# Attention scores as three products of 64 rows in the two halves of TensorE's rows

## The chip, the cores and the metric

The kernel runs on one core of a Trainium2 chip. The metric is the device time of one execution in microseconds (us). TensorE (PE in the profile, PEld for its weight loads) multiplies, VectorE (DVE), ScalarE (ACT) and GpSimd (POOL) do the rest, and all data transfers are issued from the queue of SyncE (SP, SPq).

## The reference, cut to what matters

One layer of a decoder trunk on 1024 tokens of width 1024: a projection, differential attention with four heads, an mLSTM with four heads, a gated merge, an output product. The change is in the attention alone. Each head h has two groups c of queries and keys of width 64, both turned into probabilities over the same 1024 keys:

```
scores = q[h,c] @ k[h,c].T * 64**-0.5 + alibi_bias     # c = 0, 1; causal
p      = softmax(scores)
p      = p[c=0] - lam * p[c=1]
out    = p @ v[h]
```

All inputs are float32, and the products keep nearly float32 accuracy: an operand is split into a high part that TensorE takes in one pass (type fp32r) and a low part, the rest. A product of two split operands has four terms, hi·hi, lo·hi, hi·lo and lo·lo.

## The kernel before, in words

Everything is in one function. The projection runs as `run_pairs`: 22 pairs of column blocks, each seven products of 12 matmuls of 128 rows by 512 columns (tiles named after the pair, `qka1Y`, `g00Z`, `za0X`). This is the *filler*: a generator that yields after every six matmuls. Over it lies a *chain* of small dependent steps: gate preparation, the mLSTM, then the attention heads. `weave` takes one step of the chain, then pulls as much filler as the step asks for (`yield w * FW[n]`), so that TensorE has filler to run while the chain's other engines work. The filler's total is fixed; after `run_pairs` it goes on with `merge_b`, and when the chain is over, the rest is pulled. TensorE's instructions stay in the order in which they are written from there on (`keep_in_program_order`); the framework places the other engines' instructions and the transfers.

A head is `attn_head`. For each block i of 128 queries (i = 0 to 7) it needs (i+1)·128 keys, in one segment up to 512 keys and in two equal ones beyond:

- `score(i, c)` for each group c: two matmuls per segment into one PSUM tile `S` (pool `misc`, five buffers). VectorE's reduction (L950) adds the bias from `gm`, writes the scores to `p0` or `p1` and keeps the row's extreme in `ast`; with two segments a small minimum (L956) joins them. ScalarE's exponential (L957) follows.
- `combine(i)`: VectorE forms p0 − λ·p1 (L966 to L971).
- `turn(i-1)`: transposes of the previous block's p on TensorE (`pT`), `weigh(i-1)`: the product with the values (`pv`).

In the kernel before, filler is pulled after `score(i, 0)`, after `score(i, 1)` with `combine(i)`, after `turn` and after `weigh`.

The high and low parts of q and k of each head are written by the filler to DRAM as `qk_d[h]` (qh, ql, kh, kl, each 128 rows by 1024 tokens: rows 0 to 63 are group 0, rows 64 to 127 group 1). `stacks(h)` loads them back so that the high and low parts of one group lie *on top of each other*: `qs[0]` holds qh of group 0 in rows 0 to 63 and ql of group 0 in rows 64 to 127; `khh[c]` holds kh of group c twice, `kll[c]` holds kl twice. One matmul of 128 rows then gives qh·kh + ql·kh, a second one qh·kl + ql·kl. That is 24 transfers of 64 rows by 512 tokens a head, and one for the values, `va`. Six SBUF slots (2, 3, 4, 5, 9, 10) have one home each: the next head's loads wait for the last score product of this head. `stacks(h+1)` is called in the last block (`after()`).

Of the kernel before, what the change touches and what calls it, by code (L numbers as in the profile page):

```python
# [9 lines left out]
F32 = mybir.dt.float32  # L10
F32R = mybir.dt.float32r
AF = mybir.ActivationFunctionType
ALU = mybir.AluOpType
# [3 lines left out]
P = 128  # L17
S = 1024
# [22 lines left out]
def kernel(  # L41
# [16 lines left out]
    nc = tc.nc  # L58
# [5 lines left out]
    sp = ctx.enter_context(tc.tile_pool(name="sp", bufs=2))  # L64
# [11 lines left out]
    def pin(ins):  # L76
        if ordered[0]:
            tc.keep_in_program_order(ins)

    def mm(*args, **kw):  # L80
        pin(nc.tensor.matmul(*args, **kw))  # L81

    def turn128(out, in_):
        pin(nc.tensor.transpose(out=out, in_=in_, identity=ident))  # L84
# [7 lines left out]
    def misc(name):  # L92
        return ps_m.tile([P, 512], F32, tag="m", name=name)

    def slot(i, shape, name, dtype=F32):
        return tp.tile(shape, dtype, tag=f"T{i}", name=name)
# [72 lines left out]
    for _ in range(WARM):  # L169
# [8 lines left out]
    lqk, lj, rows = scr[:, 0:256], scr[:, 256:320], scr[0:40, 320:448]  # L178
# [13 lines left out]
        out=tri, in_=ones, pattern=[[1, P]], compare_op=ALU.is_ge, fill=0.0,  # L192
# [5 lines left out]
        out=mask, in_=mask, pattern=[[1, P]], compare_op=ALU.is_ge, fill=NEG,  # L198
# [84 lines left out]
    va_d = dp.tile([4, P, NT, P], F32, name="va_d")  # L283
# [196 lines left out]
    qk_d = [dp.tile([4, P, S], F32, name=f"qk_d{h}") for h in range(4)]  # L480

    def hs_(T):
        return slice(T * 512, T * 512 + 512)
# [150 lines left out]
    for i in range(2):  # L634
        nc.vector.tensor_tensor_reduce(
            out=lj, in0=lqk[:, i * 128 : i * 128 + 64], in1=lqk[:, i * 128 + 64 : i * 128 + 128],
            scale=1.0, scalar=0.0, op0=ALU.mult, op1=ALU.add, accum_out=lam_s[:, i : i + 1],
# [260 lines left out]
        )  # L898
        return gm

    h0, h1 = slice(0, 64), slice(64, 128)

    def stacks(h):
        qs = [slot(2 + c, [P, S], f"qs{c}_{h}", F32R) for c in range(2)]
        khh = [slot(4 + c, [P, S], f"khh{c}_{h}", F32R) for c in range(2)]
        kll = [slot(9 + c, [P, S], f"kll{c}_{h}", F32R) for c in range(2)]
        va = slot(7, [P, NT, P], f"va_{h}")
        qh, ql, kh, kl = (qk_d[h][i] for i in range(4))
        for T in range(2):
            ts_ = hs_(T)  # L910
            for dst, dr, src, sr in (
                (qs[0], h0, qh, h0), (qs[0], h1, ql, h0), (khh[0], h0, kh, h0), (khh[0], h1, kh, h0),
                (kll[0], h0, kl, h0), (kll[0], h1, kl, h0), (qs[1], h0, ql, h1), (qs[1], h1, qh, h1),
                (khh[1], h0, kh, h1), (khh[1], h1, kh, h1), (kll[1], h0, kl, h1), (kll[1], h1, kl, h1),
            ):
                nc.sync.dma_start(dst[dr, ts_].bitcast(F32), src[sr, ts_])
            if T == 0:
                nc.sync.dma_start(va, va_d[h])
        return qs, khh, kll, va

    def share(i):
        return i + FB if i < NT else LAST
# [4 lines left out]
    def attn_head(h, stk, gm, supply, before, after, res):  # L927
        if h > 0:
            nc.gpsimd.tensor_scalar(gm, gm, 0.25, 0.0, ALU.mult, ALU.add)
        qs, khh, kll, va = stk  # L930
        raw = slot(8, [P, NT, P], f"oa_{h}")
        sth = sp.tile([P, 5, NT], F32, tag="sth", name=f"sth_{h}")
        live = {}

        def score(i, c):
            nk = (i + 1) * P
            if c == 0:
                live[i] = [sp.tile([P, 5], F32, tag="ast", name="ast")]
            st = live[i][0]
            pr = slot(12 if c else i % 2, [P, S], f"p{c}")  # L940
            nm = st[:, c : c + 1]
            lhs = qs[c][:, i * P : (i + 1) * P]
            seg = nk if nk <= 512 else nk // 2
            for n0 in range(0, nk, seg):
                n1 = n0 + seg
                pss = misc("S")
                part_ = nm if n0 == 0 else st[:, 4:5]
                mm(pss[:, : n1 - n0], lhs, khh[c][:, n0:n1], start=True, stop=False)
                mm(pss[:, : n1 - n0], lhs, kll[c][:, n0:n1], start=False, stop=True)
                nc.vector.tensor_tensor_reduce(  # L950
                    out=pr[:, n0:n1], in0=pss[:, : n1 - n0],
                    in1=gm[:, (7 - i) * P + n0 : (7 - i) * P + n1],
                    scale=-0.125, scalar=3.0e38, op0=ALU.add, op1=ALU.min, accum_out=part_,
                )
            if nk > 512:
                nc.vector.tensor_tensor(nm, nm, part_, ALU.min)  # L956
            nc.scalar.activation(  # L957
                pr[:, :nk], pr[:, :nk], AF.Exp, bias=nm, scale=-1.0,
                accum_out=sth[:, c, i : i + 1],
            )  # L960
            live[i].append(pr)

        def combine(i):
            nk = (i + 1) * P
            st, p0, p1 = live[i]
            nc.vector.reciprocal(st[:, 2:3], sth[:, 1, i : i + 1])  # L966
            nc.vector.scalar_tensor_tensor(
                out=st[:, 3:4], in0=sth[:, 0, i : i + 1], scalar=st[:, 2:3], in1=neglam,
                op0=ALU.mult, op1=ALU.mult,
            )  # L970
            nc.vector.scalar_tensor_tensor(  # L971
                out=p0[:, :nk], in0=p1[:, :nk], scalar=st[:, 3:4], in1=p0[:, :nk],
                op0=ALU.mult, op1=ALU.add,
            )

        def turn(i):
            p0 = live[i][1]
            pT = slot(6, [P, NT, P], "pT")
            live[i] = pT
            for j0 in range(0, i + 1, 4):  # L980
                j1 = min(i + 1, j0 + 4)
                pt = misc("pT")
                for j in range(j0, j1):
                    turn128(
                        pt[:, (j - j0) * P : (j - j0 + 1) * P], p0[:, j * P : (j + 1) * P]
                    )
                nc.scalar.copy(  # L987
                    pT[:, j0:j1], pt[:, 0 : (j1 - j0) * P].rearrange("p (j t) -> p j t", t=P)
                )

        def weigh(i):
            pT = live.pop(i)
            pv = misc("pv")
            for j in range(i + 1):
                mm(pv[:, 0:P], pT[:, j], va[:, j, :], start=(j == 0), stop=(j == i))
            nc.scalar.activation(raw[:, i], pv[:, 0:P], AF.Square, accum_out=sth[:, 2, i : i + 1])
            nc.scalar.copy(raw[:, i], pv[:, 0:P])

        unit = supply / FTOTAL
        for i in range(NT + 1):  # L1000
            w = share(i) * unit
            if i < NT:
                score(i, 0)
                yield w * FW[0]
                score(i, 1)
                combine(i)
                if i == NT - 1:
                    after()
                yield w * FW[1]
            if i > 0:  # L1010
                if i == 1 and before is not None:
                    flip(*before)
                turn(i - 1)
                yield w * FW[2]
                weigh(i - 1)
                yield w * FW[3]
        l0, ss, dd, rr = sth[:, 0, :], sth[:, 2, :], sth[:, 3, :], sth[:, 4, :]
        nc.vector.scalar_tensor_tensor(out=dd, in0=l0, scalar=EPS, in1=l0, op0=ALU.mult, op1=ALU.mult)
        nc.vector.scalar_tensor_tensor(
            out=ss, in0=ss, scalar=1.0 / P, in1=dd, op0=ALU.mult, op1=ALU.add  # L1020
        )
        nc.gpsimd.tensor_tensor(rr, ss, mhalf, ALU.pow)
        scale_rows(raw, rr, nc.gpsimd)
        res.append((raw, cols[:, 32 + h : 33 + h]))
# [94 lines left out]
    gm = build_gm()  # L1119
    stk = stacks(0)  # L1120
    before = ((mem["raw"][:, :, 0:P], cols[:, 39:40]), 7)
    flip_half(*before[0], 7, 1)
    for h in range(4):
# [12 lines left out]
        stk = global_stk[0]  # L1136
# [9 lines left out]
    for kh in range(2):  # L1146
        for T in range(2):
            for e in range(2):
                tag = (("t3h", "t3l"), ("22h", "22l"), ("t4h", "t4l"), ("11h", "11l"))[kh * 2 + T][e]
# [16 lines left out]
    for cc in range(4):  # L1166
        c0 = cc * 256
        halves = []
        for k in range(2):
            r = raw_tile([P, 4, 256], f"o{cc}{k}")  # L1170
            nc.sync.dma_start(r, w_out_v[:, k * 4 : k * 4 + 4, c0 : c0 + 256])
            t = hp.tile([P, 2, 4, 256], F32R, tag=f"h{WO[(cc * 2 + k) % 6]}", name=f"wo{cc}{k}")
            split(r, t[:, 0], t[:, 1])
            halves.append(t)
        for tt in range(NT):
            ts_ = slice(tt * P, (tt + 1) * P)
            js = slice((tt % 4) * P, (tt % 4 + 1) * P)
            ps = acc("out")
            for kt in range(KT):
                for i, (a, b) in enumerate(((0, 0), (0, 1), (1, 0))):  # L1180
# [3 lines left out]
                        start=(kt == 0 and i == 0), stop=(kt == KT - 1 and i == 2),  # L1184
# [4 lines left out]
                accum_out=ssq[:, tt, cc : cc + 1],  # L1189
# [9 lines left out]
            if cc == 3:  # L1199
                st = sp.tile([P, 3], F32, tag="ost", name="ost")  # L1200
# [3 lines left out]
                for n0 in range(0, D, 512):  # L1204
                    ns = slice(n0, n0 + 512)
                    nc.vector.scalar_tensor_tensor(
                        out=orr[:, ns], in0=orr[:, ns], scalar=st[:, 2:3], in1=xr[:, ns],
                        op0=ALU.mult, op1=ALU.add,
# [30 lines left out]
```

## Time and profile before

| | |
|---|---|
| median of 3 runs | 856.52 us (855.29 to 857.26) |
| profiled execution: time, span | 856.17 us, 854.5 us |
| granted TensorE clock | 0.995 |
| PE busy | 837.0 us, 98% |
| DVE, ACT, POOL busy | 574.1 us (67%), 403.7 us (47%), 66.0 us (8%) |
| attention stage, first to last score product | 370.0 to 677.6 us |

The profiled execution's own time is 1.7 us above the span, which counts from the first to the last instruction. PE's busy time counts each matmul from its start to the modelled end of its result, and these overlap: a row's duration of 0.39 us stands beside a distance of 0.23 us between the starts of two such matmuls. What a matmul takes from PE is read from the distance between starts.

### The profile page before, as it was taken

Reading aid. Unit: us, or ns where it says so; the run is one execution under the profiler, and the core shown is the slowest. Engines: PE = TensorE matmul, PEld = TensorE weight load, DVE = VectorE, ACT = ScalarE, POOL = GpSimd, SP = SyncE. Lnnn points to the kernel's source line nnn. Section 1 sums busy time; section 2 is a strip of 40 time slices with the busy share of each in tenths; the row PEclk is TensorE's granted clock in tenths of the full one; section 3 lists DMA queues with packets and bytes.
Section 4 is the critical chain, followed back from the end, with each engine's and each line's share of the span. In section 5 each row is a group of like instructions: output and inputs, shape, how many; then the busy total and the mean of one; then the engine's idle time right before and its main releaser. Section 6 shows DMA issues by size and latency. Waiting matters only on the chain.

```text
span 854.5 us, 13030 instructions
## 1 busy us (share of the span) xinstructions
PE 837.0 (98%) x4676; PEld 726.2 (85%) x4676; DVE 574.1 (67%) x1161; ACT 403.7 (47%) x922; POOL 66.0 (8%) x102
## 2 busy tenths in 40 slices
PE   7999999999999999999999999999999999899997
PEld 7998888888888888888888888888878888799997
DVE  5997968858768866577666764876576636872125
ACT  5554544544545444456555555565576422342111
POOL 1330000000000000100001001100200010000012
PEclk9999999999999999999999999999999999999999
DMA  8612434443342666563266326533677678820007
GB/s 265 200 38 76 124 99 111 136 148 96 124 152 68 170 182 194 164 197 115 84 179 203 123 87 211 170 125 112 196 240 252 196 248 282 302 95 1 1 26 246
DMA packets 102672, 129.00 MB, mean 151 GB/s; under 512 B 8680, under 2 KB 64208, under 8 KB 102608
## 3 DMA queue, kind: packets, MB, share of 16 engines
q1 hardware_dynamic: 102608, 128.18, 47.8%
q8 instruction: 37, 0.61, 0.3%
q14 instruction: 27, 0.22, 0.1%
HBM read 88.79 MB, written 39.35 MB: 150 GB/s over the span
## 4 chain that ended last, share of the span: by engine, by line
PE 76%; DVE 8%; DMA 7%; issue 4%; ACT 2%; SPq 1%; POOL 1%; DVEq 0%; POOLq 0%; ACTq 0%
PE out L81 9%; PE mrg L81 6%; PE S L81 3%; PE pv L81 3%; DMA m_d<-tg 2%; PE num L81 2%; PE pT L84 1%; PE tok L81 1%; PE za1Y L81 1%; PE g16Y L81 1%; PE qka3Y L81 1%; PE qka1Y L81 1%; PE g02Y L81 1%; PE za0Y L81 1%; PE zb0Y L81 1%
## 5 line engine op out<-in xcount | busy, mean ns | idle before, releaser
L81 PEld LDWEIGHTS out<-wo,m 128*128 128x128 f32 x768 | 92.3, 192 | 0.1
L81 PE MATMUL out<-wo,m 128*128 128x256 f32 x768 | 92.3, 283 | 0.0
L957 ACT ACTIVATE p<-p,ast 128x128 f32<-128x128 f32 (+7 forms) x64 | 49.6, 776 | 58.9 <-DVE ast L956 35.4
L950 DVE CUSTOM_DVE_ANT_0 p<-S,gm 128x384 f32<-128x384 f32 (+5 forms) x96 | 50.5, 553 | 21.4 <-PE S L81 20.9
L1192 DVE TENSOR_TENSOR o<-out,npost 128x256 f32<-128x256 f32 x32 | 13.5, 423 | 55.4 <-ACT oj L1187 55.4
L81 PE MATMUL mrg<-y,maw 128*128 128x512 f32 x192 | 45.7, 399 | 2.3 <-DVE tg L1084 2.3
L81 PE MATMUL mrg<-y,mbw 128*128 128x512 f32 x192 | 47.2, 395 | 0.0
L81 PEld LDWEIGHTS mrg<-y,maw 128*128 128x128 f32 x192 | 36.9, 193 | 11.0 <-DVE tg L1084 3.2
L1187 ACT ACTIVATE oj<-out 128x256 f32<-128x256 f32 x32 | 12.3, 384 | 71.2 <-PE out L81 71.2
L81 PEld LDWEIGHTS mrg<-y,mbw 128*128 128x128 f32 x192 | 35.4, 188 | 6.9
L81 PEld LDWEIGHTS pv<-va,pT 128*128 128x128 f32 x288 | 36.8, 191 | 4.5 <-ACT pT L987 2.2
L81 PE MATMUL pv<-va,pT 128*128 128x128 f32 x288 | 37.8, 276 | 0.6 <-ACT pT L987 0.5
L1084 DVE SCALAR_TENSOR_TENSOR tg<-tg,mrg 128x512 f32<-128x512 f32 x32 | 21.8, 682 | 16.2 <-PE mrg L81 13.9
L81 PE MATMUL S<-kll,qs 128*128 128x384 f32 (+5 forms) x96 | 32.7, 342 | 0.0
L81 PE MATMUL S<-khh,qs 128*128 128x384 f32 (+5 forms) x96 | 32.4, 340 | 0.0
L750 DVE SCALAR_TENSOR_TENSOR cv<-pad,cols,cv 128x1024 f32<-128x1024 f32 x24 | 30.7, 1277 | 0.1
L971 DVE SCALAR_TENSOR_TENSOR p<-p,ast,p 128x128 f32<-128x128 f32 (+7 forms) x32 | 26.2, 818 | 1.0
L851 POOL TENSOR_TENSOR stb<-stb,mhalf 128x4 f32<-128x4 f32 x8 | 10.8, 1349 | 160.7 <-DVE stb L848 160.7
L115 ACT CAST m<-tg 128x512 fp32r<-128x512 f32 x16 | 9.9, 621 | 25.6 <-DVE tg L1155 25.6
L987 ACT COPY pT<-pT 128x512 f32<-128x512 f32 (+3 forms) x48 | 21.0, 470 | 2.1 <-PE pT L84 2.0
L84 PE MATMUL pT<-ident,p 128*128 128x128 f32 x144 | 20.9, 272 | 0.0
L81 PEld LDWEIGHTS S<-kll,qs 128*128 128x128 f32 x96 | 18.0, 188 | 3.3
(1219 smaller groups left out, 2352.4 us busy)
## 6 DMA issues: line engine op xcount, KB each, us to landing
raw_g<-in_w_in_dram SPq DMA_DIRECT2D x16, 512.0 KB, 3.8
g_d<-g SPq DMA_DIRECT2D x32, 256.0 KB, 3.5
tg<-g_d SPq DMA_DIRECT2D x32, 256.0 KB, 4.2
raw_qkb<-in_w_in_dram SPq DMA_DIRECT2D x16, 256.0 KB, 3.4
z_d<-zt SPq DMA_DIRECT2D x16, 256.0 KB, 2.6
zs<-z_d SPq DMA_DIRECT2D x16, 256.0 KB, 4.7
raw_qka<-in_w_in_dram SPq DMA_DIRECT2D x16, 256.0 KB, 3.0
qk_d<-qah SPq DMA_DIRECT2D x16, 256.0 KB, 2.1
```

Of the source, the lines that this page charges most:

```text
L81: pin(nc.tensor.matmul(*args, **kw))
L84: pin(nc.tensor.transpose(out=out, in_=in_, identity=ident))
L115: nc.scalar.copy(hi, raw)
L750: nc.vector.scalar_tensor_tensor(out=cv, in0=pad[:, t : t + S], scalar=cols[:, t * 8 + blk : t * 8 + blk + 1], in1=cv, op0=ALU.mult, op1=A ...
L851: nc.gpsimd.tensor_tensor(rr, ss, mhalf[:, 0:4], ALU.pow)
L950: nc.vector.tensor_tensor_reduce(out=pr[:, n0:n1], in0=pss[:, : n1 - n0], in1=gm[:, (7 - i) * P + n0 : (7 - i) * P + n1], scale=-0.125, sc ...
L957: nc.scalar.activation(pr[:, :nk], pr[:, :nk], AF.Exp, bias=nm, scale=-1.0, accum_out=sth[:, c, i : i + 1],)
L971: nc.vector.scalar_tensor_tensor(out=p0[:, :nk], in0=p1[:, :nk], scalar=st[:, 3:4], in1=p0[:, :nk], op0=ALU.mult, op1=ALU.add,)
L987: nc.scalar.copy(pT[:, j0:j1], pt[:, 0 : (j1 - j0) * P].rearrange("p (j t) -> p j t", t=P))
L1084: nc.vector.scalar_tensor_tensor(out=tg, in0=tg, scalar=1.0, in1=ps, op0=ALU.add, op1=ALU.mult)
L1187: nc.scalar.activation(junk[:, 0:256], ps[:, 0:256], AF.Square, scale=D ** -0.5, accum_out=ssq[:, tt, cc : cc + 1],)
L1192: nc.vector.tensor_mul(orr[:, c0 : c0 + 256], ps[:, 0:256], npost[:, c0 : c0 + 256])
```

## The change

q and k are no longer stacked. The four parts are loaded as they are, each in one transfer of 128 rows by 1024 tokens, so that group 0 lies in rows 0 to 63 and group 1 in rows 64 to 127. Per segment there are three products of 64 rows for each group, qh·kh, ql·kh and qh·kl (lo·lo is left out), written alternately for group 0 and group 1, into two PSUM tiles at once. `score(i)` makes both groups; the filler that stood between the two groups stands after both. qh, kh and kl have two slots, used by even and odd heads in turn; ql and va have one. The two minima become one of two columns.

```diff
     def stacks(h):
-        qs = [slot(2 + c, [P, S], f"qs{c}_{h}", F32R) for c in range(2)]
-        khh = [slot(4 + c, [P, S], f"khh{c}_{h}", F32R) for c in range(2)]
-        kll = [slot(9 + c, [P, S], f"kll{c}_{h}", F32R) for c in range(2)]
+        tags = (2, 13)[h % 2], 3, (4, 9)[h % 2], (5, 10)[h % 2]
+        ts = [slot(t, [P, S], f"{n}_{h}", F32R) for t, n in zip(tags, ("qh", "ql", "kh", "kl"))]
         va = slot(7, [P, NT, P], f"va_{h}")
...
-                nc.sync.dma_start(dst[dr, ts_].bitcast(F32), src[sr, ts_])
-            if T == 0:
-                nc.sync.dma_start(va, va_d[h])
+        for i in (0, 2, 3, 1):
+            nc.sync.dma_start(ts[i].bitcast(F32), qk_d[h][i])
+        nc.sync.dma_start(va, va_d[h])
...
-        def score(i, c):
+        def score(i):
...
-                mm(pss[:, : n1 - n0], lhs, khh[c][:, n0:n1], start=True, stop=False)
-                mm(pss[:, : n1 - n0], lhs, kll[c][:, n0:n1], start=False, stop=True)
...
+                pss = [misc(f"S{c}")[:, :seg] for c in range(2)]
+                for n, (q, k) in enumerate(((qh, kh), (ql, kh), (qh, kl))):
+                    for c, rows in enumerate(halves_):
+                        mm(pss[c], q[rows, qs_], k[rows, n0:n1], start=n == 0, stop=n == 2)
+                for c in range(2):
+                    part_ = st[:, c : c + 1] if n0 == 0 else st[:, 4 + c : 5 + c]
+                    nc.vector.tensor_tensor_reduce(
...
+            if nk > 512:
+                nc.vector.tensor_tensor(st[:, 0:2], st[:, 0:2], st[:, 4:6], ALU.min)
+            for c in range(2):
+                nc.scalar.activation(
...
-                score(i, 0)
+                score(i)
                 yield w * FW[0]
-                score(i, 1)
                 combine(i)
```

On TensorE, block 3 of head 0 (512 keys, one segment). Before, the two groups' products stand apart, with five matmuls of the pair `qka1X` between them (`S` is the scores' PSUM tile, the last numbers tell buffers apart):

```order
L81 MATMUL S<-khh_0_3654,qs_0_3652 128x512
L81 MATMUL S<-kll_0_3656,qs_0_3652 128x512
L81 MATMUL qka1X<-h21h,qka1w_3785 128x512
L81 MATMUL qka1X<-h21l,qka1w_3785 128x512
L81 MATMUL qka1X<-h21h,qka1w_3785 128x512 x2
L81 MATMUL S<-khh_0_3655,qs_0_3653 128x512
L81 MATMUL S<-kll_0_3657,qs_0_3653 128x512
```

The same block after, on TensorE, where S_3849 is group 0 (rows 0 to 63 of both operands) and S_3850 group 1 (rows 64 to 127):

```order
L81 MATMUL qka1X<-h21h,qka1w_3767 128x512
L81 MATMUL S_3849<-kh_3654,qh_3652 128x512
L81 MATMUL S_3850<-kh_3654,qh_3652 128x512
L81 MATMUL S_3849<-kh_3654,ql_3653 128x512
L81 MATMUL S_3850<-kh_3654,ql_3653 128x512
L81 MATMUL S_3849<-kl_3655,qh_3652 128x512
L81 MATMUL S_3850<-kl_3655,qh_3652 128x512
L81 MATMUL qka1X<-h21h,qka1w_3767 128x512
```

The four matmuls of 128 rows in two stretches have become six of 64 rows in one stretch, with matmuls of 128 rows on both sides of it. Over the four heads there are 192 score matmuls in 61 stretches before, and 288 in 33 stretches after.

On SP's queue, the end of the loads for head 1. Before, 24 loads of `qs`, `khh` and `kll` and the values' load `va` stand nearly in a row; behind them come the filler's stores `z_d` and `g_d` and the load `zs`, on which the flip of the last head's output waits (L573):

```order
L916 DMA qs_1_4309<-qk_d_159 64x512 x2
L916 DMA khh_1_4311<-qk_d_159 64x512
L918 DMA va_4314<-va_d 128x1024
L916 DMA khh_1_4311<-qk_d_159 64x512
L916 DMA kll_1_4313<-qk_d_159 64x512 x2
L528 DMA z_d<-zt 128x512
L539 DMA g_d<-g 128x512
L573 DMA zs<-z_d 128x512
L394 DMA raw_va_4641<-in_w_in_dram 128x4x256
```

After, on SP's queue, the loads for head 1 from the second one on (the load of qh stands three rows ahead):

```order
L910 DMA kh_4308<-qk_d_159 128x1024
L528 DMA z_d<-zt 128x512
L910 DMA kl_4309<-qk_d_159 128x1024
L400 DMA raw_qka_4349<-in_w_in_dram 128x4x128 x2
L400 DMA raw_qka_4352<-in_w_in_dram 128x4x128 x2
L528 DMA z_d<-zt 128x512
L910 DMA ql_4307<-qk_d_159 128x1024
L528 DMA z_d<-zt 128x512 x2
L573 DMA zs<-z_d 128x512
L394 DMA raw_va_4623<-in_w_in_dram 128x4x256
L539 DMA g_d<-g 128x512
L911 DMA va_4310<-va_d 128x1024
```

Four loads take the place of 24, the filler's transfers stand between them, and the first `zs` now stands ahead of the values' load.

More of the change, by code (lines that the diff above doesn't have):

```diff
@@ L899, in build_gm @@
         return gm
-    h0, h1 = slice(0, 64), slice(64, 128)
+    halves_ = slice(0, 64), slice(64, 128)
     def stacks(h):
-        qs = [slot(2 + c, [P, S], f"qs{c}_{h}", F32R) for c in range(2)]
-        khh = [slot(4 + c, [P, S], f"khh{c}_{h}", F32R) for c in range(2)]
-        kll = [slot(9 + c, [P, S], f"kll{c}_{h}", F32R) for c in range(2)]
+        tags = (2, 13)[h % 2], 3, (4, 9)[h % 2], (5, 10)[h % 2]
+        ts = [slot(t, [P, S], f"{n}_{h}", F32R) for t, n in zip(tags, ("qh", "ql", "kh", "kl"))]
         va = slot(7, [P, NT, P], f"va_{h}")
[L908 to L916, printed above, removed]
-            if T == 0:
-                nc.sync.dma_start(va, va_d[h])
-        return qs, khh, kll, va
+        for i in (0, 2, 3, 1):
+            nc.sync.dma_start(ts[i].bitcast(F32), qk_d[h][i])
+        nc.sync.dma_start(va, va_d[h])
+        return *ts, va
     def share(i):
@@ L929, in attn_head @@
             nc.gpsimd.tensor_scalar(gm, gm, 0.25, 0.0, ALU.mult, ALU.add)
-        qs, khh, kll, va = stk
+        qh, ql, kh, kl, va = stk
         raw = slot(8, [P, NT, P], f"oa_{h}")
@@ L933, in attn_head @@
         live = {}
-        def score(i, c):
+        def score(i):
             nk = (i + 1) * P
[L937 to L942, printed above, removed]
+            st = sp.tile([P, 6], F32, tag="ast", name="ast")
+            ps_ = slot(i % 2, [P, S], "p0"), slot(12, [P, S], "p1")
+            live[i] = [st, *ps_]
@@ L943, in score @@
             seg = nk if nk <= 512 else nk // 2
+            qs_ = slice(i * P, (i + 1) * P)
             for n0 in range(0, nk, seg):
                 n1 = n0 + seg
-                pss = misc("S")
-                part_ = nm if n0 == 0 else st[:, 4:5]
-                mm(pss[:, : n1 - n0], lhs, khh[c][:, n0:n1], start=True, stop=False)
-                mm(pss[:, : n1 - n0], lhs, kll[c][:, n0:n1], start=False, stop=True)
[L950 to L953, printed above, removed]
-                )
@@ L955, in score @@
[L955 to L961, printed above, removed]
+                pss = [misc(f"S{c}")[:, :seg] for c in range(2)]
+                for n, (q, k) in enumerate(((qh, kh), (ql, kh), (qh, kl))):
+                    for c, rows in enumerate(halves_):
+                        mm(pss[c], q[rows, qs_], k[rows, n0:n1], start=n == 0, stop=n == 2)
@@ new lines, in score @@
+                for c in range(2):
+                    part_ = st[:, c : c + 1] if n0 == 0 else st[:, 4 + c : 5 + c]
+                    nc.vector.tensor_tensor_reduce(
+                        out=ps_[c][:, n0:n1], in0=pss[c],
+                        in1=gm[:, (7 - i) * P + n0 : (7 - i) * P + n1],
+                        scale=-0.125, scalar=3.0e38, op0=ALU.add, op1=ALU.min, accum_out=part_,
+                    )
+            if nk > 512:
+                nc.vector.tensor_tensor(st[:, 0:2], st[:, 0:2], st[:, 4:6], ALU.min)
@@ L963, in combine @@
+            for c in range(2):
+                nc.scalar.activation(
+                    ps_[c][:, :nk], ps_[c][:, :nk], AF.Exp, bias=st[:, c : c + 1], scale=-1.0,
+                    accum_out=sth[:, c, i : i + 1],
+                )
         def combine(i):
```

## The prediction

> **What bounds the kernel now.** I read the page first, its busy times and the chain of waits, then the attention stage alone, since the change is there.
>
> ```profile
> span 854.5 us, 13030 instructions
> PE 837.0 (98%) x4676; PEld 726.2 (85%) x4676; DVE 574.1 (67%) x1161; ACT 403.7 (47%) x922; POOL 66.0 (8%) x102
> PE 76%; DVE 8%; DMA 7%; issue 4%; ACT 2%; SPq 1%; POOL 1%; DVEq 0%; POOLq 0%; ACTq 0%
> ```
>
> The chain runs over PE for 76% of the span; the other engines have slack. For the stage of the four heads the view by stretches gives PE's busy time (343.25 of 345 us); PE's waits there are in the list of waits:
>
> ```profile
> 355.00:700.00 345.00, 343.25 (x1786) 290.48 (x1785) 231.15 (x542) 191.92 (x450) 24.18 (x18) 1.00 0.55 173
> PE g00Y L81 <- DVE g L537: 0.6, 1, 0.6
> PEld pv L81 <- ACT pT L987: 2.2, 5, 0.9
> PEld g00Y L81 <- DVE g L537: 0.9, 1, 0.9
> PEld g06X L81 <- DVE g L537: 0.9, 1, 0.9
> ```
>
> So in this stage time is what PE's stream of matmuls takes. The filler is a fixed amount of work, so a microsecond more or less of score products is a microsecond of the end; what other engines save counts only where it shortens one of these few waits.
>
> **What the score products take now.** A busy row overlaps with its neighbours, so I take distances between starts, from the timeline of PE: the first score matmul of a stretch and the first matmul behind the stretch (in the first group also the one ahead).
>
> ```profile
> 448.56 0.40 PE L81 MATMUL g00Z<-ht1h,g00w 128*128 128x512 f32 x1
> 448.79 0.22 PE L81 MATMUL S<-khh,qs 128*128 128x128 f32 x1
> 448.96 0.44 PE L81 MATMUL g00Z<-ht1h,g00w 128*128 128x512 f32 x1
> ...
> 373.62 0.28 PE L81 MATMUL S<-khh,qs 128*128 128x256 f32 x1
> 373.85 0.39 PE L81 MATMUL g16Y<-ht3h,g16w 128*128 128x512 f32 x1
> ...
> 395.46 0.31 PE L81 MATMUL S<-khh,qs 128*128 128x320 f32 x1
> 396.06 0.39 PE L81 MATMUL qka1Y<-ht3h,qka1w 128*128 128x512 f32 x1
> ...
> 406.23 0.34 PE L81 MATMUL S<-khh,qs 128*128 128x384 f32 x1
> 406.93 0.39 PE L81 MATMUL qka1Y<-ht4h,qka1w 128*128 128x512 f32 x1
> ...
> 417.62 0.36 PE L81 MATMUL S<-khh,qs 128*128 128x448 f32 x1
> 418.44 0.39 PE L81 MATMUL za0Z<-ht1h,za0w 128*128 128x512 f32 x1
> ...
> 429.49 0.39 PE L81 MATMUL S<-khh,qs 128*128 128x512 f32 x1
> 430.41 0.40 PE L81 MATMUL g00Y<-h11h,g00w 128*128 128x512 f32 x1
> ```
>
> Two matmuls lie between the first two pairs of rows, four between the others. One matmul takes 0.085 us at 128 keys, 0.115 at 256, 0.15 at 320, 0.175 at 384, 0.205 at 448 and 0.23 at 512. By the loop the four heads have 16, 16, 32, 48, 32 and 48 of them: 1.4 + 1.8 + 4.8 + 8.4 + 6.6 + 11.0 = 34.0 us.
>
> **Part 1: the products (−6.6 us, between −8.2 and −2.0).** There are 288 matmuls in 144 pairs, 12, 12, 24, 36, 24 and 36 by the number of keys. The two of a pair read different partitions, use different rows of the array and write different PSUM tiles, and stand next to each other. No row of before shows whether such two run at the same time; I take it that they do, and price the opposite as a rival. What a pair costs then hangs on its two weight loads. The trace shows one load (128 columns) to the next at no less than about 0.11 us, and fewer rows don't shorten it: two loads of 32 rows, each 0.18 long, fill 0.29 us together, so they start 0.11 apart (78.44 below). If the two loads of a pair go side by side, a pair costs the distance above, 0.11 at least: 1.3 + 1.4 + 3.6 + 6.3 + 4.9 + 8.3 = 25.8 us, a gain of 8.2. If they go one after the other, a pair costs at least 0.22: 108 × 0.22 + 8.3 = 32.0, a gain of 2.0. That row is of the same rows of the array twice and stands no nearer to one end than to the other, so I take the middle, 0.165 us at least for a pair: 48 × 0.165 + 6.3 + 4.9 + 8.3 = 27.4 us, a gain of 6.6.
>
> On this the Trainium skill has a rule ("TensorE: Matmul & The Clock Gate", Part 3, the mechanism): matmuls on different row groups run concurrently, with starts about 4 ns apart, and loads overlap where the row groups differ. By it the gain is the full 8.2 us; no run here shows it so far.
>
> **Part 2: changing between 128 and 64 rows (+13.2 us, between 0 and 16.8).** Every stretch of score products now has matmuls of 128 rows on both sides. The trace of before has such changes at two places early on: a transpose of 40 rows (`rowsT`) and two products of 32 rows (`mu`).
>
> ```profile
> 68.43 0.28 PE L81 MATMUL tok<-wc,h22h 128*128 128x256 f32 x1
> 68.64 0.14 PEld L87 LDWEIGHTS rowsT<-ident,scr 40*128 40x128 f32 x1
> 68.64 0.25 PE L87 MATMUL rowsT<-ident,scr 40*128 40x40 f32 x1
> 68.82 0.19 PEld L81 LDWEIGHTS qkb0Y<-h11h,qkb0w 128*128 128x128 f32 x1
> ...
> 78.01 0.50 PE L81 MATMUL qkb0Z<-ht1h,qkb0w 128*128 128x512 f32 x1
> 78.44 0.29 PEld L81 LDWEIGHTS mu<-ident,gs 32*128 32x128 f32 x2 [0.25 <-issue]
> 78.44 0.40 PE L81 MATMUL mu<-ident,gs 32*128 32x32 f32 x2
> 78.77 0.19 PEld L81 LDWEIGHTS qkb0Z<-ht1l,qkb0w 128*128 128x128 f32 x1
> 78.77 0.50 PE L81 MATMUL qkb0Z<-ht1l,qkb0w 128*128 128x512 f32 x1
> 78.88 0.19 PEld L81 LDWEIGHTS qkb0Z<-ht1h,qkb0w 128*128 128x128 f32 x1
> ```
>
> Among matmuls of 128 rows the next load starts under the running matmul (78.88, 0.11 behind the start of 78.77). Where the number of rows changes, the load waits until 0.07 us before the recorded end of the matmul ahead: 68.71 against 68.64, 68.89 against 68.82, 78.51 against 78.44, 78.84 against 78.77. The wait of 0.25 at 78.44 is put down to no semaphore. The filler's matmul of 512 columns lasts 0.39 us and is followed by the next after 0.23; with a change the next starts after 0.39 − 0.07 = 0.32, 0.09 later. And the load that then stands in the open costs its 0.11: the matmul behind it lasts 0.50, not 0.39. Entering costs 0.20 us. Leaving does too: a score matmul of 384 columns lasts 0.34, the load comes at 0.27, not 0.175, and stands open. With 0.40 us for each of the 33 stretches that is 13.2 us. Nothing covers it: it is PE's own time. The upper end puts the pair's second load behind the first on entering, 0.11 × 33 = 3.6 more. The lower end is nothing, if 64 rows, half of the array, were handled unlike 32 and 40; the nearest row, the 40, speaks against it.
>
> The Trainium skill ("TensorEngine Tiling (Array Packing)", Key Properties) says that changing the tiling mode drains TensorE, and that tiles of one mode load and multiply in parallel. By that rule, the trace agrees in the four rows above, and within a stretch no drain is due; its sum is 13.2 − 8.2, a loss of 5.0 us before part 3.
>
> **Part 3: loads, queue and waits (−1.0 us, between −1.8 and 0).** 24 loads a head become four; a load took about 0.6 us of SP's queue:
>
> ```profile
> 435.84 1.24 SPq L916 DMA_DIRECT2D khh<-qk_d  x2
> ...
> 448.46 1.94 SPq L916 DMA_DIRECT2D kll<-qk_d  x2
> ...
> 457.62 0.43 SPq L573 DMA_DIRECT2D zs<-z_d  x1
> ```
>
> The load of `zs` comes late behind them, and VectorE, which takes its work in order, comes late to the `g` on which PE waits (0.9 us, above). With the shorter queue this wait and that of g06X may go, 1.8 us, or both may stay, since `va` still waits for the last `pv`; I take 1.0. The loads themselves are hidden by filler now (before each head's first score, PE goes on at its usual distance: 448.56 to 448.79 in the same timeline), and two homes make them earlier still. `ql` has one home and waits for the last score product, `va` for the last `pv`, as in before.
>
> VectorE and ScalarE do the same reductions and exponentials; the four reductions of a block now come in a row. One small minimum less per long block is nothing. In the stage VectorE is busy 231 of 345 us (first fence of the stage), so this is covered as long as PE has filler to run behind `score(i)`, which it has.
>
> **The sum.** −6.6 + 13.2 − 1.0 = +5.6 us on the profiled execution's 856.17 is 861.8; that execution is 0.35 below the median of 856.52, so 862.
>
> **Rivals.** The third needs the page's row of the reductions, 0.55 us each.
>
> ```profile
> L950 DVE CUSTOM_DVE_ANT_0 p<-S,gm 128x384 f32<-128x384 f32 (+5 forms) x96 | 50.5, 553 | 21.4 <-PE S L81 20.9
> ```
>
> 1. *The change of rows costs nothing, or little, for halves of 64.* Then −8.2 to −6.6 and −1.0 remain: 847 to 849 us, faster. For it: only 40 and 32 rows are seen, in two places. Against: all four boundaries there give the same 0.07. It decides from the point where a stretch costs under (6.6 + 1.0) / 33 = 0.23 us instead of 0.40.
> 2. *The halves do not run together; the change does not do what it says.* Then 288 matmuls each take their distance: 24 × 0.11 + 24 × 0.115 + 48 × 0.15 + 72 × 0.175 + 48 × 0.205 + 72 × 0.23 = 51.6 us, 17.6 more than now; with the changes of rows and part 3 that is 856.5 + 17.6 + 13.2 − 1.0 = 886 us. For it: no row of before has two matmuls in less than their distance. Against: different rows, different partitions, different PSUM tiles.
> 3. *PSUM.* A long block takes four of the five `misc` buffers at once; if others hold two, PE waits for a reduction, 0.55 us and more for a long one, in each of 16 long blocks: some 10 us on top, 872. Against: filler stands between a block's scores and its neighbours' `pT` and `pv`, longer than the reductions take.
>
> **Chances.** Halves together with drains, 0.62, of which a few hundredths end within 0.2%; rival 1, 0.20, some of it with half a drain, near no change; rival 2, 0.14; rival 3, 0.04. The likeliest case's own range is 860 (side by side, less 1.8 of waits: −8.2 + 13.2 − 1.8 = +3.2) to 871 (one after the other, with 16.8: −2.0 + 16.8 = +14.8). The range that leaves out rival 2 and rival 1's last microsecond is 848 to 872. Faster by over 0.2% 0.20, within 0.2% (what a measurement here can hardly tell from no change) 0.08, slower 0.72.
>
> **What would show it.** In the profile after: the two matmuls of a pair start close together, not 0.23 us apart, and the next pair follows at the distance of one (part 1); a filler matmul ahead of a stretch is followed after 0.32 us and the first one behind it lasts about 0.50 (part 2); PE's wait at g00Y is gone (part 3); PE stays at 98%. I am wrong if the pairs stand two distances apart (time near 886) or if the loads at the borders of a stretch start under the matmul ahead (time below 850).

## The result, and the profile after

The changed kernel takes 865.75 us (median of 4 runs, 863.84 to 869.37) against 855.90 us for the kernel before in the same comparison (4 runs): ratio 1.0117, 95% interval 1.0092 to 1.0141, so 8 to 12 us slower. The profiled execution took 869.37 us, its span is 867.7. From the page after, the span, the busy times and the chain of waits:

```profile
span 867.7 us, 13085 instructions
PE 844.1 (97%) x4772; PEld 716.7 (83%) x4772; DVE 573.6 (66%) x1145; ACT 400.6 (46%) x922; POOL 66.6 (8%) x102
PE 76%; DVE 8%; DMA 8%; issue 3%; ACT 3%; SPq 1%; POOL 1%; DVEq 0%; POOLq 0%; ACTq 0%
```

PE still carries the chain with 76%; nothing else has become the bound. PE's busy share is 97%, not the 98% that was foreseen. The timeline of PE and its weight loads at block 2 of head 0 (384 keys, one stretch) answers to the rows of before at 406.23 and at 78.01 to 78.88:

```profile
386.10 0.40 PE L81 MATMUL qka1Y<-h11h,qka1w 128*128 128x512 f32 x1
386.42 0.19 PEld L81 LDWEIGHTS S<-kh,qh 64*128 64x128 f32 x2 [0.36 <-issue]
386.42 0.44 PE L81 MATMUL S<-kh,qh 64*128 64x384 f32 x2
386.53 0.19 PEld L81 LDWEIGHTS S<-kh,ql 64*128 64x128 f32 x2
386.71 0.34 PE L81 MATMUL S<-kh,ql 64*128 64x384 f32 x2
386.71 0.19 PEld L81 LDWEIGHTS S<-kl,qh 64*128 64x128 f32 x2
386.88 0.35 PE L81 MATMUL S<-kl,qh 64*128 64x384 f32 x2
387.15 0.19 PEld L81 LDWEIGHTS qka1Y<-h11h,qka1w 128*128 128x128 f32 x1 [0.26 <-issue]
387.15 0.50 PE L81 MATMUL qka1Y<-h11h,qka1w 128*128 128x512 f32 x1
387.49 0.40 PE L81 MATMUL qka1Y<-h11l,qka1w 128*128 128x512 f32 x1
```

Three things stand in these ten rows. A pair (x2) takes the time of one: from 386.71 to 386.88 is 0.17 us, what one matmul of 384 columns took before. The two loads of a pair go side by side: two loads of 0.19 us are over in 0.19. And both borders are open: the first load comes 0.32 us behind the filler's start, not under it, 386.42 to 386.71 is 0.29 instead of 0.17 since the load is in it, and the filler behind the stretch lasts 0.50 and is followed after 0.34, not 0.23.

One thing I had not looked for is at head 0's start. From the list of PE's waits in the attention stage, and the view by stretches of 370.5 to 382 us (the columns are the stretch, its length, PE, PEld, DVE, ACT and POOL busy with their instructions, granted clock, DMA share, GB/s):

```profile
PE S L81 <- DMA kl<-qk_d: 2.3, 1, 2.3
PE g02Z L81 <- ACT g_p L349: 1.8, 1, 1.8
PEld S L81 <- DMA kl<-qk_d: 2.7, 1, 2.7
370.50:382.00 11.50, 9.19 (x35) 6.41 (x33) 5.26 (x18) 3.19 (x10) 0.00 (x0) 0.70 0.38 130
```

PE stands still for head 0's `kl`, and the granted clock of the stretch is 0.70. The timeline of SP's queue, with PE's rows at both ends, shows why:

```profile
365.35 0.39 PE L81 MATMUL num<-cn,qi 128*128 128x129 f32 x2
365.59 0.32 SPq L911 DMA_DIRECT2D va<-va_d  x1
366.71 0.32 SPq L539 DMA_DIRECT2D g_d<-g  x1
367.47 0.32 SPq L560 DMA_DIRECT2D va_d<-tko  x1
367.88 0.43 SPq L910 DMA_DIRECT2D kl<-qk_d  x1
...
371.37 0.39 PE L81 MATMUL g16Z<-ht1l,g16w 128*128 128x512 f32 x1
374.07 0.47 PE L81 MATMUL S<-kl,qh 64*128 64x128 f32 x2 [2.31 <-DMA kl<-qk_d]
374.47 1.22 PE L81 MATMUL g16Z<-ht1h,g16w 128*128 128x512 f32 x2
375.49 0.63 PE L81 MATMUL g16Z<-ht1l,g16w 128*128 128x512 f32 x1
375.92 0.63 PE L81 MATMUL g16Z<-ht1h,g16w 128*128 128x512 f32 x1
```

`kl` of head 0 lies in slot 5, where the mLSTM keeps `qi`; its last reader is the product `num` at 365.35. On the queue the values' load stands ahead, with two of the filler's stores. The load is issued at 367.88 and PE can go on at 374.07, though it wanted the data at about 371.6. Before, the second operand lay in slots 9 and 10 and came in pieces.

The list has a second wait that is new, of 1.8 us for `g_p` (L349) at 597.8 us, and the clock is low behind it too (in the same 10 us of the kernel before PE is busy throughout, at a clock of 1.00):

```profile
594.00:604.00 10.00, 8.24 (x38) 6.97 (x37) 5.48 (x11) 5.86 (x14) 0.00 (x0) 0.83 0.21 49
```

### The profile page after: what moved, and what is told of

It reads as the page before. It is cut to its first block, busy times and chain, and to the rows that moved or that the text cites. A ratio compares the mean times of both kernels' runs of the same rounds, so it can differ in the third digit from the quotient of the medians.

```text
span 867.7 us, 13085 instructions
## 1 busy us (share of the span) xinstructions
PE 844.1 (97%) x4772; PEld 716.7 (83%) x4772; DVE 573.6 (66%) x1145; ACT 400.6 (46%) x922; POOL 66.6 (8%) x102
## 4 chain that ended last, share of the span: by engine, by line
PE 76%; DVE 8%; DMA 8%; issue 3%; ACT 3%; SPq 1%; POOL 1%; DVEq 0%; POOLq 0%; ACTq 0%
PE out L81 8%; PE mrg L81 5%; PE pv L81 3%; PE S L81 3%; DMA m_d<-tg 3%; PE num L81 1%; PE pT L84 1%; PE qka3Y L81 1%; PE qka2Y L81 1%; PE qka1Y L81 1%; PE za1Y L81 1%; PE tok L81 1%; PE qkb0Y L81 1%; PE zb0Y L81 1%; PE ob1Y L81 1%
## 5 line engine op out<-in xcount | busy, mean ns | idle before, releaser
L989 ACT ACTIVATE oa<-pv 128x128 f32<-128x128 f32 x32 | 8.8, 276 | 25.6 <-PE pv L81 25.6
L84 PEld LDWEIGHTS pT<-ident,p 128*128 128x128 f32 x144 | 17.5, 140 | 3.5
L819 ACT ACTIVATE junk<-raw 128x128 bf16<-128x128 f32 x32 | 9.8, 307 | 22.8 <-DVE raw L814 22.7
```

## The experiments

All but the fused block (e5) rest on one edit, the first one, so that head 0's wait doesn't stand in the comparison. e3 and e4 leave out products and don't compute the whole result.

**Other homes for k (e1).**

```diff
-        tags = (2, 13)[h % 2], 3, (4, 9)[h % 2], (5, 10)[h % 2]
+        tags = (2, 13)[h % 2], 3, (4, 5)[h % 2], (9, 10)[h % 2]
```

> The changed kernel with other homes for k's parts: kl of even heads goes to slot 9, kh of odd heads to slot 5, so that head 0's kl no longer waits for the slot in which the mLSTM keeps qi, nor stands behind the values' load. Theory (the loss is 33 changes of rows at 0.40 us, less 8.2 us of products, plus head 0's wait for kl of 2.7 us and the slower clock behind it, some 3 us): PE's wait for kl goes, the granted clock stays at 1.00 there, 859 to 861 us, some 6 us under the changed kernel. Rival (that wait is taken back later, since PE catches up on filler): no change from 866.

The median is 862.4 us (862.0 without the profiled execution, whose 1947 us are left out of the ratio), ratio to before 1.0045 (1.003 to 1.006): 2.6 to 5.1 us slower than before, on 858.07, where the changed kernel is 8 to 12 slower. The same kernel once more, for a profile:

> The same kernel as e1_home, once more, because that profile lasted 1945 us and says nothing of the timed runs. By the theory of 33 changes at 0.40 us and a free second half: each stretch as in the changed kernel, no wait for kl, granted clock 1.00 behind it. It ran 3 us behind e2_in_turn, which has the same matmuls in another order; if that is real, PE's waits outside the stretches differ; if it is chance, the two agree within 1 us here.

861.45 us, ratio 1.0034 (1.0015 to 1.0053). The same stretch of time by the view by stretches:

```profile
370.50:382.00 11.50, 11.50 (x62) 8.85 (x62) 9.33 (x25) 6.37 (x19) 0.00 (x0) 1.00 0.42 132
```

No wait, the granted clock at 1.00, and 62 matmuls where the changed kernel has 35. The rival, that PE takes the wait back later, is out: 1.0117 has become 1.0034 to 1.0045, some 6 to 7 us. At head 0 the trace of the changed kernel accounts for 5.7 of them: PE's wait of 2.3 us, and 30% of 11.5 us, 3.4, by the low clock, in which the filler's matmuls stood 0.43 us apart instead of 0.23 (375.49 to 375.92 above). The wait for `g_p` has shrunk as well, from 1.8 to 0.4 us (in the list under e3), and the clock from 588 to 604 us is 1.00 here. Whether that follows from the late `kl` was not tried, so 6 to 7 us is the price of the whole edit, and one late transfer is shown for 5.7.

**The two groups in turn (e2).**

```diff
-                for n, (q, k) in enumerate(((qh, kh), (ql, kh), (qh, kl))):
-                    for c, rows in enumerate(halves_):
+                for c, rows in enumerate(halves_):
+                    for n, (q, k) in enumerate(((qh, kh), (ql, kh), (qh, kl))):
                         mm(pss[c], q[rows, qs_], k[rows, n0:n1], start=n == 0, stop=n == 2)
```

> As e1_home, but the three products of group 0 are written ahead of the three of group 1, instead of alternately. Theory (two matmuls run together only where neighbours in the queue use different rows): five of six neighbours now share their rows, so a segment takes close to six distances instead of three, less the one overlap: 15 to 18 us more than e1_home, about 877. Rival (the queue looks far enough ahead to pair them): the same as e1_home within 2 us.

858.91 us, ratio 1.0011 (0.9992 to 1.0029). The theory that neighbours in the program must use different rows is refuted. In the timeline of block 4 (320 keys, first of two segments) the matmuls stand in pairs as in the changed kernel, though in the program, whose order is pinned, the three of group 0 come first:

```profile
396.58 0.42 PE L81 MATMUL S<-kh,qh 64*128 64x320 f32 x2
396.83 0.32 PE L81 MATMUL S<-kh,ql 64*128 64x320 f32 x2
396.98 0.32 PE L81 MATMUL S<-kl,qh 64*128 64x320 f32 x2
397.13 0.31 PE L81 MATMUL S<-kh,qh 64*128 64x320 f32 x2
```

Group 1's first matmul is fourth in the program and starts with group 0's first; the second segment begins at 397.13, after three distances.

The rival's number did not hold either: e2 is some 3 us faster than e1 in the same comparison, and 2.5 by the medians than e1's second run, where chance was to leave 1 us at most. The stretches don't differ (38.4 us against 38.2, added up as under e3), and PE's waits in the stage hardly do (1.8 us against 1.9). Of the 2.4 us between the two profiled spans (856.4 and 858.8), 1.1 lie ahead of the first score product (370.4 and 371.5), where the two programs are the same. What makes the medians differ stays open.

e2 is also nearer to the kernel before than its stretches say: they take 3.5 us more, the profiled span is only 1.9 longer (856.4 against 854.5). A difference stands behind the attention. The kernel before waits 2.3 us there for VectorE's `tg` (L1084), e2 1.4 us, and by the view by stretches the granted clock of before is lower (first row before, second row e2):

```profile
728.00:740.00 12.00, 9.73 (x36) 7.92 (x37) 11.09 (x18) 3.80 (x7) 0.00 (x0) 0.86 0.88 300
728.00:740.00 12.00, 10.62 (x47) 8.44 (x47) 10.33 (x17) 4.48 (x7) 0.00 (x0) 1.00 0.96 301
```

0.14 of 12 us is 1.7 us, about what is missing. One execution of each shows this; whether the others do too is not shown.

**One half alone (e3).**

```diff
-                pss = [misc(f"S{c}")[:, :seg] for c in range(2)]
+                pss = [misc("S0")[:, :seg]] * 2
...
-                    for c, rows in enumerate(halves_):
-                        mm(pss[c], q[rows, qs_], k[rows, n0:n1], start=n == 0, stop=n == 2)
+                    mm(pss[0], q[halves_[0], qs_], k[halves_[0], n0:n1], start=n == 0, stop=n == 2)
```

> As e1_home, but group 1's three products of each segment are left out; both groups' reductions read group 0's scores. 144 products of 64 rows instead of 288, the same 32 stretches. Theory (the second half of a pair is free): within 2 us of e1_home. Rival (the halves run together only in part, or the two weight loads of a pair go one after the other): 4 to 18 us faster than e1_home.

856.81 us, ratio 0.9979 (0.9963 to 0.9995): by the ratios 5.7 us less than e1 and 4.7 less than its second run, more than the 2 I gave and, by its number, what the rival said. But the difference is not in the stretches, where the rival puts it. I add up over all of them the distance from the filler's matmul ahead to the second one behind, less these two's own distances: 38.1 us here, 38.2 in e1's second run, with half the matmuls. What differs is outside: here PE has no wait for another engine in the stage, while e1 has

```profile
PE pv L81 <- ACT pT L980: 1.5, 2, 0.9
PE g02Z L81 <- ACT g_p L349: 0.4, 1, 0.4
```

These are 1.9 us of the 2.7 between the two profiled spans (858.8 and 856.1); for the rest of the difference no cause is shown. The kernel also takes half as many PSUM buffers for scores. Whether that is what ends these waits was not tried.

**All rows (e4).**

```diff
-                    mm(pss[0], q[halves_[0], qs_], k[halves_[0], n0:n1], start=n == 0, stop=n == 2)
+                    mm(pss[0], q[:, qs_], k[:, n0:n1], start=n == 0, stop=n == 2)
```

> As e3_one_half, but the remaining 144 products use all 128 rows (which adds the two groups' scores up, and leaves group 1's own out): the same columns, loads and order, and no change of rows. Theory (a change of rows costs 0.40 us a stretch): 32 x 0.40 = 12.8 us faster than e3_one_half, about 847. Rival (the changes of rows are covered, and the loss comes from the fused block or the waits): the same as e3_one_half within 2 us.

846.38 us, ratio 0.9871 (0.9841 to 0.9901), 10.4 us less than e3; foreseen were 12.8. Block 3 (512 keys) of head 0 in the two kernels, first of 64 rows, then of 128, from the timelines of PE:

```profile
388.34 0.39 PE L81 MATMUL qka1X<-h21h,qka1w 128*128 128x512 f32 x1
388.66 0.50 PE L81 MATMUL S<-kh,qh 64*128 64x512 f32 x1
389.00 0.39 PE L81 MATMUL S<-kh,ql 64*128 64x512 f32 x1
389.23 0.39 PE L81 MATMUL S<-kl,qh 64*128 64x512 f32 x1
389.55 0.51 PE L81 MATMUL qka1X<-h21h,qka1w 128*128 128x512 f32 x1
389.89 0.40 PE L81 MATMUL qka1X<-h21l,qka1w 128*128 128x512 f32 x1
```

```profile
387.38 0.40 PE L81 MATMUL qka1X<-h21h,qka1w 128*128 128x512 f32 x1
387.62 0.39 PE L81 MATMUL S<-kh,qh 128*128 128x512 f32 x1
387.85 0.40 PE L81 MATMUL S<-kh,ql 128*128 128x512 f32 x1
388.08 0.39 PE L81 MATMUL S<-kl,qh 128*128 128x512 f32 x1
388.32 0.39 PE L81 MATMUL qka1X<-h21h,qka1w 128*128 128x512 f32 x1
388.55 0.40 PE L81 MATMUL qka1X<-h21l,qka1w 128*128 128x512 f32 x1
```

The same five distances take 1.55 us with 64 rows and 1.17 with 128: 0.38 for entering and leaving. Over all stretches the score products take 38.1 and 26.0 us, 12.1 for 32 stretches, again 0.38. The end shows 10.4 of these; e4's profile has 1.3 us of PE's waits in the stage, e3's has none.

**The fused block alone (e5).** The kernel before, with only its order changed:

```diff
                 score(i, 0)
-                yield w * FW[0]
                 score(i, 1)
+                yield w * FW[0]
```

> The kernel before, with its stacked products of 128 rows, and only one thing taken from the change: both groups' scores stand in one stretch, with the filler behind them. Theory (the fused block costs nothing, the changes of rows do): within 2 us of the kernel before. Rival (four reductions in a row delay the filler's, and PE waits): 3 to 8 us slower.

857.09 us against 857.64, ratio 0.9994 (0.9983 to 1.0005). Both groups in one stretch cost nothing. The rival is out.

**More stretches (e6).** The filler behind a long block's scores is halved, and one half stands between the segments (`score` becomes a generator):

```diff
+                if n1 < nk:
+                    yield
...
-                score(i)
-                yield w * FW[0]
+                f0 = FW[0]
+                for _ in score(i):
+                    f0 = FW[0] / 2
+                    yield w * f0
+                yield w * f0
```

> As e2_in_turn, with half of the filler that stood behind a long block's scores put between its two segments: 46 stretches of score products instead of 32. Theory (0.40 us a stretch): 14 x 0.40 = 5.6 us slower than e2_in_turn. Rival (a change of rows is mostly covered): within 2 us of it.

865.8 us, ratio 1.0094 (1.0073 to 1.0116), about 7 us more than e2. The stretches take 44.7 us instead of 38.4, 6.3 for 14 more, 0.45 each. Besides, one long wait is in this profile, and a low clock behind it:

```profile
PE pv L81 <- ACT pT L982: 2.6, 1, 2.6
652.00:661.00 9.00, 6.37 (x27) 4.53 (x27) 5.15 (x8) 6.99 (x14) 0.00 (x0) 0.81 0.57 201
```

**Fewer stretches (e7).** Blocks 0 and 1, and 2 and 3, share a stretch:

```diff
+        pair_p = []
...
-            ps_ = slot(i % 2, [P, S], "p0"), slot(12, [P, S], "p1")
+            if i < 4 and i % 2:
+                ps_ = [t[:, 512:] for t in pair_p]
+            else:
+                ps_ = slot((i // 2 if i < 4 else i) % 2, [P, S], "p0"), slot(12, [P, S], "p1")
+                pair_p[:] = ps_
...
-                score(i)
+                if i > 3:
+                    score(i)
+                elif i % 2 == 0:
+                    score(i)
+                    score(i + 1)
```

> As e2_in_turn, with the scores of blocks 0 and 1, and of 2 and 3, in one stretch (their p0 and p1 share a tile each): 24 stretches instead of 32. Theory: 8 x 0.40 = 3.2 us faster than e2_in_turn, and so about 2 us faster than the kernel before. Rival (longer stretches make PE wait for the reductions to give PSUM buffers back): no faster than e2_in_turn.

859.5 us, ratio 1.0022 (1.0009 to 1.0035): no faster than e2. The stretches give what was foreseen, 35.4 us instead of 38.4 for 8 fewer, 0.38 each; but it doesn't reach the end. Of PE's waits in the stage, the first row is this kernel's and the second is e2's:

```profile
PE pv L81 <- ACT pT L985: 2.1, 2, 1.7
```

```profile
PE pv L81 <- ACT pT L980: 1.0, 2, 0.6
```

That is 1.1 us of what is missing. Another 1.7 are lost behind the attention: in this profile PE's wait for `tg` (L1085) there is 1.9 us, and the granted clock from 728 to 740 us is 0.86, as in the kernel before, where e2 has 1.00 (its row stands under e2):

```profile
728.00:740.00 12.00, 10.05 (x38) 7.67 (x37) 9.81 (x16) 4.47 (x7) 0.00 (x0) 0.86 0.91 300
```

The rest is not settled. No version tried that computes the whole result beats the kernel before.

## Why the prediction was right, step by step

The sign and the range held: 862 was forecast in 848 to 872, 865.75 was measured. The sum was +5.6 us, the ratio says +8 to +12. That the two are this near is partly luck: parts 1 and 2 were forecast some 3 us too slow, part 3 some 7 us too fast, and the two errors offset each other in part.

- **Part 1, the products.** Forecast −6.6, the middle between loads side by side (−8.2) and one after the other (−2.0). The score stretches of before take 34.9 us, and 26.0 for three products without a change of rows (e4): −8.9, near the 8.2 of loads side by side. The loads of a pair go side by side, so my middle was the mis-sized term; the trace after shows it in the first x2 row of loads. That the second half is free, which I took without a row, is shown by e3's stretches, 38.1 against 38.2 us. Rival 2 (886 us) is refuted by the same.
- **Part 2, the changes of rows.** Forecast 0.40 us for each of 33 stretches, 13.2; measured 0.38 (e3 against e4) and 12.1 for 32 stretches, 0.45 and 0.38 when stretches were added (e6) and taken away (e7). Four borders of 32 and 40 rows in the gate preparation had priced 64 rows to 0.02 us. Rival 1 (no drain) is refuted; e4's 846 us is about what the change would have given then, as the second half is free, near the 847 to 849 that stood there.
- **Parts 1 and 2 together** are 38.2 − 34.9 = +3.3 us, and e1, the change without head 0's wait, is 2.9 to 3.9 us slower than before by its two ratios. By the stretches the drains (the open borders on entering and leaving) are thus slightly dearer than the products are cheaper; how much of it reaches the end moves with what happens outside them (e2, with the same matmuls, lies between 0.7 us faster and 2.5 slower than before). A long block of 512 keys a segment gains two distances, 0.46 us, and pays 0.38; a block of one segment gains at most 0.23.
- **Part 3, loads and waits.** Forecast −1.0, between −1.8 and 0: the wrong sign. The step that failed is "The loads themselves are hidden by filler now", with "two homes make them earlier still". I read it from a row at head 1's start and let it stand for all heads. The waits at g00Y and g06X did go, as forecast, but others came: without head 0's wait, PE's waits in the stage are 1.9 us (e1), against 1.5 before (0.6 and 0.4 for these two, 0.5 for pT), so the gain of 1.0 did not come either. And head 0's `kl` got another home, with a late last reader, and a late place on the queue: 6 to 7 us with what followed, as e1 shows by taking that away. I had moved a transfer and not asked for each slot who reads it last.
- **Rival 3, PSUM.** Nothing like the 10 us given. In no profile of these kernels does the list of PE's waits have a score product that waits for a reduction to give its buffer back, and the fused block by itself (e5) costs nothing. Waits for `pT` come and go by 1 to 3 us between the kernels (e1, e3, e6, e7); what sets them was not tried.

The Trainium skill's two rules of the prediction stand as far as runs show them: by "TensorEngine Tiling (Array Packing)", Key Properties, a change of mode drains, and tiles of one mode load and multiply in parallel; the trace agrees with both, at 0.38 us for a stretch and 0.17 us for a pair of 384 columns.

## What to carry to other kernels

Using half of the rows for each of two independent products makes the second one free, but count the stretches, not only the matmuls: with other matmuls of all rows on both sides each stretch paid 0.38 us here, so it gains only where a stretch saves clearly more than that. Price such a border from any small matmul of few rows that the trace already has. When a tile gets another home, ask for every user, the first one too, who reads the old contents last and what stands ahead of its load on the queue.

## What the runs showed of the hardware that was not expected

Matmuls of the two row halves did not need to be neighbours: with three of group 0 written ahead of three of group 1, the pairs started together all the same (396.58 above), and after the first pair, which has the open load ahead of it, the pairs followed 0.15 us apart, the distance of one matmul of 320 columns.

A wait of 2.3 us on PE was followed by a stretch with a granted clock of 0.70, and cost 5.7 us, more than twice the wait. Waits of 1.8 us (the changed kernel, `g_p`), 1.9 (e7, `tg`), 2.3 (before, `tg`) and 2.6 (e6, `pT`) also stand beside stretches at 0.81 to 0.86, but one of 1.7 us (e7, `pT`, at 633) does not: the clock from 632 to 640 us is 1.00.
